# First block of a two-block network: a gate chunk moved ahead of the gated-delta drain, side work stepped later, first weight units split between two norms

## The chip, the cores and the metric

The program runs on one core of a Trainium2 chip. A core has five engines with a queue of instructions each, which run on their own and meet through semaphores: TensorE (PE; PEld is its weight load), VectorE (DVE), ScalarE (ACT), GpSimd (POOL) and SyncE (SP), which here only issues DMAs. The metric is the device time of one execution in microseconds (us); lower is better. The median over several runs counts.

## What is computed

256 tokens of width 1024 go through a first block of two layers (`first0`, `first1`), a final norm, and a second block of six phases (swiglu, hybrid mixer, swiglu, swiglu, recurrent mixer, swiglu). The change lies in the first block alone. One layer of it is, cut to what matters:

```python
h = rms_norm(x, norm_g[l])
gu, gv, gz, rq, rk, rv, rz, dq, dk, dv, dz, ab... = split(h @ w_in[l])
y_a = gmlp_branch(gu, gv, gz, ...)        # gelu, layer norm of v, mixing over tokens, gate z
y_b = retention_branch(rq, rk, rv, rz, ...)
y_c = gdn_branch(dq, dk, dv, dz, ab...)   # gated delta rule: triangular solves (I + L)^-1, states
proj  = einsum("bsnw,nwd->bsnd", stack(y_a, y_b, y_c), w_branch_out[l])
gates = sigmoid(einsum("bsd,dne->bsne", h, w_gate[l]))
x = x + sum(gates * proj, axis=2) @ w_out[l]
```

## The kernel before, in words

All weights stream through one queue of **units** of 128 x 1024 floats (`unit`, L280): SP issues the load of a unit into `st`, ACT rounds it into `wh` (L277), DVE makes the remainder `wl = st - wh` (L278). Products are made three times (`mm3`: high by high, high by low, low by high), so a unit costs 12 matmuls of 512 columns: six for each of the two token tiles. Five raw and six split units are in flight (`NS`, `NW`).

`xs` (L305) makes one chunk of 512 columns, with the tokens on the partitions: for each unit a **half unit** (six matmuls) for token tile 0 and one for tile 1. After each half unit `step` (L238) advances the **side work**: every queue of generators (`gdn`, `gm`, `ret`, `load`) by one `yield`, and functions that were put aside by `hold` for so many half units. So the place of a side instruction among the weight matmuls is counted in yields. Within each engine the instructions run in the order in which they stand; PE's, DVE's and ACT's order is made by a scheduler when the program is built, POOL's is the order in which the code is written (`tc.manual_schedule` for Pool in `run`, L538).

The first block's layer (`first`, L660) has three branches:

- **Retention**, side work in the queue `ret`. Its last step takes a power on POOL (`rsr<-rsv,mhalf` of 128 x 8, L414) for the row factors of `ro`, which DVE applies.
- **Gated MLP** (`gmlp`, L809). The chunk `v` is passed through gelu into `tB`; `mean_rstd` takes its mean and variance on DVE and a power on POOL (`rsr<-rsv,mhalf` of 128 x 1, once per token tile). The generator `mix` (queue `gm`) waits `YA` = 6 yields, normalizes `tB` on DVE, waits two yields, and multiplies by `gsw` on PE: the four matmuls `sm<-tB,gsw` per token tile, called the **gsw group** below.
- **Gated delta rule** (`gdn_core`, L969, queue `gdn`). It makes the triangular matrices L and stores their diagonal blocks (`gdl<-g`), loads them with one block per partition (`gv<-gdl`, called X), and inverts them on POOL alone, column by column: for j = 1 to 30 a product (`gtx<-gv`, L1063) and a sum (`gv<-gv,gtx`, L1065) of (31-j) x j elements, one yield per j. Then X goes out to memory (`gdt<-gv`), comes back as whole matrices (`g<-gdt`), DVE transposes these (`g<-g`, STREAM_TRANSPOSE, L1091), and PE doubles the size of the inverted blocks twice: the **g group** `gd<-g,g` (eight matmuls of 64 columns for a chunk of tokens), a mask on DVE (`gY<-gd,cst`), the **gY group** `gd<-gY,g`, a subtraction, transposes `gd<-ci,g`. Solves, states and outputs follow.

The branches' outputs meet in `merge` (L765): for a branch and a half of the columns one chunk of the gate (four units) and one chunk of the branch's projection (two units). `merge(yb, .)` is for retention, `merge(gm[3], .)` for the gated MLP, `merge(yc, .)` for the gated delta rule. `drain("gdn")` (L720) runs what is left of the side work before the chunk `dz` (`cd`), which gates that branch's output `od`; `branch_T(..., n)` transposes a branch's output n half units later.

At the start, `run` norms and transposes both token tiles, `prep(0)` and `prep(1)`, and then the weight stream begins.

Of the kernel before, what the change touches and what calls it, by code (L numbers as in the profile page):

```python
# [19 lines left out]
# half units of the weight stream before the constants are loaded, and before the use of a norm's factors  # L20
NY = 12
YA, YB = 6, 6
# column chunks of a swiglu computed with the tokens on the partitions
FX = 2
# weight units in flight: split ones, and ones as they come in
NW, NS = 6, 5
# units that the second token tile runs behind
LO, LF, LH, LR = 4, 6, 4, 5
# matmuls that bring up the tensor engine's clock
# [3 lines left out]
# columns of the constant pack  # L33
# [4 lines left out]
# rows of the broadcast pack  # L38
B_FIN, B_PN, B_LN, B_RG, B_SSM, B_IN = 0, 1, 7, 9, 11, 12
# columns of the small vector pack  # L40
V_L, V_DTB, V_ALOG, V_D, V_FB, V_N = 24, 48, 64, 80, 96, 104
# columns of the per-channel pack
# [37 lines left out]
def host_layout(i, phases=PHASES):  # L80
    i = {k: np.asarray(v) for k, v in i.items()}
    seg = []
    for ph in phases:
        if ph.startswith("first"):
# [9 lines left out]
            seg += [pieces(dz)] + mg(0, CS[1]) + mg(2, CS[0]) + mg(2, CS[1])  # L94
# [56 lines left out]
def bcl(ap, n):  # L151
    """[128, a] -> [128, a, n] along a new last axis."""
    return ap.unsqueeze(ap.ndim).to_broadcast(list(ap.shape) + [n])


def bcm(ap, n):
    """[128, a] -> [128, n, a] along a new middle axis."""
    return ap.unsqueeze(1).to_broadcast([ap.shape[0], n] + list(ap.shape[1:]))
# [10 lines left out]
class Net:  # L169
    def __init__(self, tc, a, out, phases):  # L170
        self.tc, self.nc, self.a, self.out = tc, tc.nc, a, out
        self.phases = phases
        self.wi = 0
        self.pend = deque()
        self.lag = 0
        self.bg = {}
        self.held = deque()
        self.zeroed = False
        self.ready = False

# [35 lines left out]
    def later(self, fn):  # L216
        """queue work of the second token tile, which runs `lag` units behind the first."""
# [8 lines left out]
    def spawn(self, queue, gen):  # L226
        """side work, advanced by one yield per half unit of the weight stream, in order per queue."""
        self.bg.setdefault(queue, deque()).append(gen)

    def hold(self, fn, n=3):  # L230
        """fn a few half units later, so that its matmuls don't wait for the work before them."""
# [19 lines left out]
    def turns(*gens):  # L251
        """one yield of each in turn."""
# [16 lines left out]
    def tr4(self, srcs, tag="sm"):  # L269
        """transposes of [128, 128] blocks into one bank."""  # L270
# [9 lines left out]
    def unit(self, g=None):  # L280
        """next weight unit as (hi, lo), each [128, 1024]; its rows (two k-tiles) scaled by g."""
# [23 lines left out]
    def xs(self, cb, lhs=None, nk=8):  # L305
        """one 512-column chunk; lhs(k, t) gives the (hi, lo) of k-tile k; cb(t, psum [128, 512])."""
# [20 lines left out]
    def outp(self, lhs, nk, cb):  # L327
        """all 1024 columns; cb(t, c, psum) for half c. The last units of the second token tile go by halves."""
# [27 lines left out]
    def ws(self, evac, pair=None):  # L356
        """one 512-column chunk, transposed: evac(f, psum[128 columns, 256 tokens]),
        or pair(f // 2, psum[128 columns, 2, 256]).

        Two column tiles share a bank: the first matmul into the bank clears its flags for both."""  # L360
# [25 lines left out]
    def small_proj(self, src, n, out):  # L386
        """side work: a few columns of the input projection, PSUM [128, 2, n] appended to out."""
# [21 lines left out]
    def pw(self, o, i):  # L409
        """i ** -0.5"""  # L410
# [18 lines left out]
    def prep_open(self, ph, tag="bcn"):  # L429
        """tiles for the transposed input of phase ph; returns prep(t, scratch [128, 1024]).  # L430

        A swiglu has the norm's gain in its weights, and takes the row factor when it leaves PSUM."""
# [22 lines left out]
        def prep(t, h):  # L455
# [15 lines left out]
            if ffn:  # L471
                # half the row factor, and 4 eps over its square for the norm after the swiglu
# [10 lines left out]
    def post(self, ph, half, prep, tag="h"):  # L483
        """x += (0.5 if half) * rms_norm(out, g), then the next phase's input.

        After a swiglu out still lacks its row factor, which is in the eps instead."""
# [26 lines left out]
    def log1pexp(self, x, shape, tag):  # L513
        """log(1 + exp(-|x|)) by 2 atanh(u / (2 + u)), u = exp(-|x|) <= 1."""
# [23 lines left out]
    def run(self):  # L538
        tc, nc, a = self.tc, self.nc, self.a
        with (  # L540
            # GDN's blocks take GpSimd turns with the powers of the norms, as traced
# [8 lines left out]
            # for the diagonal blocks of GDN's systems, and of their inverses in a matrix of zeros  # L550
# [12 lines left out]
            # loads the function table while x is on its way  # L563
            self.act(cp.tile([128, 1], F32, tag="first", name="first"), self.mhalf[:, :1], AF.Tanh)
            nc.sync.dma_start(self.x[0], a["x"][TS[0]])
            with tc.tile_pool(name="start", bufs=1) as self.ph:
# [3 lines left out]
                # the tensor engine's clock is up by the time x is there  # L570
                z, warm = self.t("z", [128]), self.sm()
                nc.vector.memset(z, 0.0)
                for n in range(WARM):
                    self.mm(warm[:, :128], z, z, start=True, stop=True)
                for t in range(2):
                    prep(t, self.t("h", [1024], bufs=2))
            if not self.phases[0].startswith("first"):
# [31 lines left out]
    def ffn(self, ph, nxt):  # L609
        """silu(r a) b, with the row factor r of the norm; the second r is left to the next norm."""  # L610
        self.lag = LF
        hid = []
        for c in range(FX):
            hid.append([[self.t(f"a{n}{c}{t}", [2, 128], F32R) for n in "hl"] for t in range(2)])

            def cb(t, ps, c=c):
                # silu(r a) = (tanh(r a / 2) + 1) r a / 2
# [42 lines left out]
    def first(self, l, nxt):  # L660
# [58 lines left out]
        self.merge(gm[3], m, 0)  # L719
        self.drain("gdn")  # L720
# [3 lines left out]
        def cd(t, ps):  # L724
# [6 lines left out]
            self.branch_T(yc, t, of, 14)  # L731

        self.xs(cd)
        self.merge(gm[3], m, 1)
# [30 lines left out]
    def merge(self, y, m, c, new=False):  # L765
        """m += 2 * sigmoid(gate) * (y @ w_branch_out), half c of the columns."""
# [18 lines left out]
    def silu2(self, p, tag="gate", bufs=3):  # L785
        """2 * silu of a PSUM tile."""
# [22 lines left out]
    def gmlp(self, l):  # L809
        """callbacks of the chunks u, v and z, and the branch's output."""  # L810
# [13 lines left out]
        def mix(t, mv, r):  # L824
# [3 lines left out]
            for _ in range(1 if t else YA):  # L828
# [22 lines left out]
    def rot(self, dst, w):  # L851
        """rotary embedding of a chunk of four heads, transposed into dst."""
# [116 lines left out]
    def gdn_core(self, G):  # L969
        """side work; a yield after every group of matmuls, the two chunks taking turns."""  # L970
# [11 lines left out]
        # sums of squares of q and k: [128 tokens, (q, k), chunk, head]  # L982
# [14 lines left out]
        # coefficients, [128, chunk, dir, head]  # L997
# [10 lines left out]
        # L (lower, unit diagonal left out) and masked scores P, per chunk and direction  # L1008
# [29 lines left out]
        # a diagonal block of 32 per partition: inverse of (I + block), column by column in its place  # L1038
# [12 lines left out]
        # decays over a chunk: 0: fwd to the row (incl.), 1: fwd from the row, 2, 3: mirrored  # L1051
# [5 lines left out]
        ea, eb = [ex[:, 0], ex[:, 2]], [ex[:, 1], ex[:, 3]]  # L1057
        nc.gpsimd.tensor_scalar(X, X, -1.0, None, op0=MUL)
        tx = self.t("gtx", [256])[:64]
        for j in range(1, 31):  # L1060
# [5 lines left out]
            yield  # L1066
        nc.gpsimd.memset(X.rearrange("p i j -> p (i j)")[:, ::33], 1.0)
# [3 lines left out]
        # inverses of (I + L): T = TN and its transpose TT, doubling the size of the diagonal blocks  # L1071
# [13 lines left out]
        for _ in range(3):  # L1085
# [32 lines left out]
        # solves, states and outputs  # L1118
# [430 lines left out]
```

## Time and profile before

| | us |
|---|---|
| median of 3 runs | 1747.17 |
| lowest and highest | 1743.41, 1748.79 |
| the profiled execution's span | 1749.0 |
| PE busy | 1702.5 (97%) |
| DVE busy, ACT busy | 1194.5 (68%), 884.3 (51%) |
| POOL busy | 159.3 (9%) |
| layer `first0` on the trace, about | 0 to 345 |
| layer `first1`, about | 345 to 672 |

PE is the engine that is busy nearly all the time; times with `<-` in a row name what released a waiting engine. The granted TensorE clock (PEclk) is a share of full speed: 1.00 is 2.4 GHz, 0.50 is 1.2 GHz. The mean over the span is 0.982.

### The profile page before, as it was taken

The numbers are of one execution on the slowest core, as the hardware profiler recorded it, in microseconds if no ns is written. First come the engines' busy times: TensorE is split into PE (matmuls) and PEld (weight loads), VectorE is DVE, ScalarE is ACT, GpSimd is POOL, SyncE is SP. The second block draws the span as 40 slices with busy tenths as digits, with TensorE's granted clock in tenths as the row PEclk, the third lists the DMA queues.
The fourth block names the chain that finished last, engine by engine and source line by source line (L and its number), as shares of the span: only waits on it lengthen the run. The fifth ranks groups of instructions, "written<-read, shape, count | busy, mean of one in ns | idle before, by whom it ended". The sixth has DMA issues, their size and how long they took to land.

```text
span 1749.0 us, 26736 instructions
## 1 busy us (share of the span) xinstructions
PE 1702.5 (97%) x10312; PEld 1504.4 (86%) x10312; DVE 1194.5 (68%) x1941; ACT 884.3 (51%) x1387; POOL 159.3 (9%) x207
## 2 busy tenths in 40 slices
PE   9998999999989999999999999999999999999998
PEld 8986888797878887998799888999789987979986
DVE  6887466688765667774568766865587647987743
ACT  5543244454513447553465455653475535875532
POOL 0058000001830000000000000000000000000000
PEclk9999899999979999999999999999999999999999
DMA  8455336464543455654454335754565545447542
GB/s 303 150 163 180 111 113 199 158 203 131 171 138 110 155 182 201 214 184 149 171 181 157 107 110 175 254 186 157 180 237 185 182 154 195 157 146 227 183 156 74
DMA packets 83279, 296.80 MB, mean 170 GB/s; under 512 B 9680, under 2 KB 10320, under 8 KB 83152
## 3 DMA queue, kind: packets, MB, share of 16 engines
q1 hardware_dynamic: 81360, 289.85, 49.9%
q0 software_dynamic: 1792, 5.24, 1.1%
q8 instruction: 81, 1.33, 0.3%
q14 instruction: 46, 0.38, 0.1%
HBM read 290.33 MB, written 4.72 MB: 169 GB/s over the span
## 4 chain that ended last, share of the span: by engine, by line
PE 80%; POOL 6%; DVE 5%; ACT 3%; DMA 3%; issue 2%; SPq 0%; POOLq 0%; DVEq 0%; ACTq 0%
PE mm L198 70%; PE gd L198 6%; POOL gv L1065 2%; POOL gtx L1063 2%; PE sm L273 2%; PE sm L198 2%; POOL rsr L414 1%; DMA st<-in_wst_dram 1%; DVE wl L192 1%; DVE wl L278 1%; ACT wh L277 1%; PE gd L273 1%; DVE x L192 1%; ACT wh L195 1%; DMA gdt<-gv 1%
## 5 line engine op out<-in xcount | busy, mean ns | idle before, releaser
L278 DVE TENSOR_TENSOR wl<-st,wh 128x1024 fp32r<-128x1024 f32 x348 | 430.8, 1244 | 276.3 <-ACT wh L277 275.4
L277 ACT CAST wh<-st 128x1024 fp32r<-128x1024 f32 x348 | 363.8, 1049 | 446.4 <-PE mm L198 420.0
L198 PE MATMUL mm<-hh,wh 128*128 128x256 f32 x1664 | 473.8, 285 | 0.0
L198 PE MATMUL mm<-hl,wh 128*128 128x256 f32 x1664 | 471.6, 283 | 0.0
L198 PE MATMUL mm<-hh,wl 128*128 128x256 f32 x1664 | 471.1, 283 | 0.0
L198 PEld LDWEIGHTS mm<-hh,wh 128*128 128x128 f32 x1664 | 319.1, 192 | 2.0 <-issue 1.2
L198 PEld LDWEIGHTS mm<-hl,wh 128*128 128x128 f32 x1664 | 317.4, 191 | 1.5 <-issue 1.2
L198 PEld LDWEIGHTS mm<-hh,wl 128*128 128x128 f32 x1664 | 317.4, 191 | 1.2 <-issue 1.0
L192 DVE SCALAR_TENSOR_TENSOR wl<-st,ci,wh 128x512 fp32r<-128x512 f32 x352 | 251.3, 747 | 78.7 <-ACT wh L195 78.6
L195 ACT ACTIVATE wh<-st,ci 128x512 fp32r<-128x512 f32 x352 | 234.2, 716 | 105.9 <-PE mm L198 84.2
L198 PE MATMUL mm<-wh,hh 128*128 128x512 f32 x656 | 272.2, 417 | 2.2 <-ACT wh L277 2.1
L198 PE MATMUL mm<-wh,hl 128*128 128x512 f32 x656 | 262.6, 401 | 0.0
L198 PE MATMUL mm<-wl,hh 128*128 128x512 f32 x656 | 260.1, 397 | 0.0
L198 PEld LDWEIGHTS mm<-wh,hh 128*128 128x128 f32 x656 | 125.7, 192 | 26.8 <-ACT wh L277 2.4
L198 PEld LDWEIGHTS mm<-wh,hl 128*128 128x128 f32 x656 | 125.5, 191 | 27.0 <-issue 0.5
L198 PEld LDWEIGHTS mm<-wl,hh 128*128 128x128 f32 x656 | 125.5, 191 | 24.2 <-issue 1.4
L198 PE MATMUL mm<-wl,ah 128*128 128x512 f32 x352 | 138.9, 394 | 0.0
L414 POOL TENSOR_TENSOR rsr<-rsv,mhalf 128x1 f32<-128x1 f32 (+1 forms) x32 | 29.0, 906 | 1204.4 <-DVE rsv L192 954.5
L198 PE MATMUL mm<-wh,ah 128*128 128x512 f32 x352 | 138.4, 393 | 0.0
L198 PE MATMUL mm<-wh,al 128*128 128x512 f32 x352 | 138.3, 393 | 0.0
L198 PEld LDWEIGHTS mm<-wh,ah 128*128 128x128 f32 x352 | 65.9, 187 | 15.8
L198 PEld LDWEIGHTS mm<-wh,al 128*128 128x128 f32 x352 | 65.9, 187 | 15.5
(386 smaller groups left out, 2041.9 us busy)
## 6 DMA issues: line engine op xcount, KB each, us to landing
st<-in_wst_dram SPq DMA_DIRECT2D x524, 512.0 KB, 3.5
bcp<-in_bc_dram SPq DMA_DIRECT2D x7, 512.0 KB, 5.2
gdl<-g POOLq DMA_DIRECT2D x8, 256.0 KB, 2.8
cst<-in_bc_dram SPq DMA_DIRECT2D x4, 512.0 KB, 4.8
g<-gdt POOLq DMA_DIRECT2D x8, 256.0 KB, 4.4
bcn<-in_bc_dram SPq DMA_DIRECT2D x3, 512.0 KB, 5.4
x<-in_x_dram SPq DMA_DIRECT2D x2, 512.0 KB, 4.9
cst<-in_cst_dram SPq DMA_DIRECT2D x4, 256.0 KB, 4.6
```

Source lines behind the costliest of these rows:

```text
L192: self.nc.vector.scalar_tensor_tensor(o, a, s, b, op0=op0, op1=op1)
L195: self.nc.scalar.activation(o, i, f, **k)
L198: self.nc.tensor.matmul(*a, **k)
L273: self.nc.tensor.transpose(p[:, j], s, self.ident)
L277: self.nc.scalar.copy(hi, src)
L278: self.nc.vector.tensor_sub(lo, src, hi)
L414: self.nc.gpsimd.tensor_tensor(o, i, self.mhalf[:, :i.free_size()], op=ALU.pow)
L1063: nc.gpsimd.tensor_tensor(u, X[:, j + 1:, j:j + 1].to_broadcast([64, n, j]), X[:, j:j + 1, :j].to_broadcast([64, n, j]), op=MUL)
L1065: nc.gpsimd.tensor_tensor(X[:, j + 1:, :j], X[:, j + 1:, :j], u, op=ADD)
```

## The change

It does six things, in both layers except for the last:

1. The second gate and projection of the gated MLP, `merge(gm[3], m, 1)`, come before `drain("gdn")` and the chunk `dz` instead of after them (the weight stream's order on the host follows).
2. `gdn_core` yields ten times more: three times before the first POOL instruction on X, once after each odd j with (31-j) x j over 200 (j = 11, 13, ... 21: six), and once more before `chain`.
3. `mix` waits 10 yields instead of 6 (`YA`), and 2 instead of 1 for the second tile.
4. The transposes of the third branch's output are held 5 half units instead of 14.
5. The docstrings and comments go (left out below).
6. At the very start, three weight units are loaded and split after `prep(0)` and before `prep(1)`; `unit` hands them out later.

```diff
-YA, YB = 6, 6
+YA, YB = 10, 6
...
-            seg += [pieces(dz)] + mg(0, CS[1]) + mg(2, CS[0]) + mg(2, CS[1])
+            seg += mg(0, CS[1]) + [pieces(dz)] + mg(2, CS[0]) + mg(2, CS[1])
...
+        self.pre = deque()
...
     def unit(self, g=None):
+        if self.pre:
+            return self.pre.popleft()
...
+                self.ui = self.xn = 0
                 for t in range(2):
                     prep(t, self.t("h", [1024], bufs=2))
+                    if t == 0 and self.phases[0].startswith("first"):
+                        first = [self.unit() for _ in range(3)]
+                self.pre.extend(first)
...
         self.merge(gm[3], m, 0)
+        self.merge(gm[3], m, 1)
         self.drain("gdn")
...
-            self.branch_T(yc, t, of, 14)
+            self.branch_T(yc, t, of, 5)
 
         self.xs(cd)
-        self.merge(gm[3], m, 1)
         self.merge(yc, m, 0)
...
-            for _ in range(1 if t else YA):
+            for _ in range(2 if t else YA):
                 yield
...
         ea, eb = [ex[:, 0], ex[:, 2]], [ex[:, 1], ex[:, 3]]
+        for _ in range(3):
+            yield
         nc.gpsimd.tensor_scalar(X, X, -1.0, None, op0=MUL)
...
             nc.gpsimd.tensor_tensor(X[:, j + 1:, :j], X[:, j + 1:, :j], u, op=ADD)
             yield
+            if n * j > 200 and j % 2:
+                yield
...
-        for _ in range(3):
+        for _ in range(4):
             yield
 
         def chain(c):
```

Where the instructions stand is shown for three places of `first0`; `first1` has the same pattern (its first power stands after j = 9 before and after j = 6 now, its two other ones follow j = 17 now).

POOL, inversion of X: `gtx` is the product and `gv` the sum of one j, and the free sizes give (31-j) x j; `rsr` of 128 x 8 is retention's power, `rsr` of 128 x 1 the gated MLP's. Before, retention's stands after j = 8 and the gated MLP's first one after j = 22:

```order
L1063 TENSOR_TENSOR gtx<-gv 64x184
L1065 TENSOR_TENSOR gv<-gv,gtx 64x23x8
L414 TENSOR_TENSOR rsr<-rsv,mhalf 128x8
L1063 TENSOR_TENSOR gtx<-gv 64x198
...
L1063 TENSOR_TENSOR gtx<-gv 64x198
L1065 TENSOR_TENSOR gv<-gv,gtx 64x9x22
L414 TENSOR_TENSOR rsr<-rsv,mhalf 128x1
L1063 TENSOR_TENSOR gtx<-gv 64x184
```

Now the same engine and place:

```order
L1074 TENSOR_TENSOR gv<-gv,gtx 64x26x5
L417 TENSOR_TENSOR rsr<-rsv,mhalf 128x8
L1072 TENSOR_TENSOR gtx<-gv 64x150
...
L1072 TENSOR_TENSOR gtx<-gv 64x240
L1074 TENSOR_TENSOR gv<-gv,gtx 64x15x16
L417 TENSOR_TENSOR rsr<-rsv,mhalf 128x1
L1072 TENSOR_TENSOR gtx<-gv 64x238
```

Retention's power moved forward to behind j = 5, the gated MLP's first one to behind j = 16.

PE, the side groups among the weight matmuls (`mm<-...`, left out as "..."), from the first gsw group to the first g groups. Before:

```order
L198 MATMUL sm<-tB,gsw 128x128 x4
...
L273 MATMUL gd<-ci,g_635 128x128 x2
...
L198 MATMUL sm<-tB,gsw 128x128 x4
...
L198 MATMUL gd<-g_1765,g_979 128x64 x4
L198 MATMUL gd<-g_1767,g_985 128x64 x4
...
L198 MATMUL gd<-gY,g_1675 128x64 x4
```

Now:

```order
L199 MATMUL sm<-tB,gsw 128x128 x4
...
L274 MATMUL gd<-ci,g_635 128x128 x2
...
L199 MATMUL gd<-g_1867,g_979 128x64 x4
L199 MATMUL gd<-g_1869,g_985 128x64 x4
...
L199 MATMUL gd<-g_1883,g_1055 128x64 x4
L199 MATMUL gd<-g_1885,g_1061 128x64 x4
...
L199 MATMUL gd<-gY,g_1773 128x64 x4
```

The first gsw group stands 24 weight matmuls later than before, and from it to the first g group there are now 78 weight matmuls, two gsw and two transpose groups (before: 47 weight matmuls and the same four groups). In `first1` these are 24 and 72.

DVE, from the transposes of the inverses to the first mask `gY`. Before:

```order
L1091 STREAM_TRANSPOSE g_1765<-g_1675 128x512
L1091 STREAM_TRANSPOSE g_1767<-g_1677 128x512
L1091 STREAM_TRANSPOSE g_1782<-g_1679 128x512
L278 TENSOR_TENSOR wl<-st,wh 128x1024
L1091 STREAM_TRANSPOSE g_1784<-g_1681 128x512
L183 TENSOR_TENSOR gY<-gd,cst 128x512
```

Now:

```order
L1102 STREAM_TRANSPOSE g_1885<-g_1779 128x512
L279 TENSOR_TENSOR wl<-st,wh 128x1024
L193 SCALAR_TENSOR_TENSOR gate<-gate,mm 128x512
L184 TENSOR_TENSOR ggm<-gv,grv 128x512
L193 SCALAR_TENSOR_TENSOR tA<-tA,gate 128x512
L193 SCALAR_TENSOR_TENSOR gate<-gate,mm 128x512
L279 TENSOR_TENSOR wl<-st,wh 128x1024
L193 SCALAR_TENSOR_TENSOR tA<-tA,gate 128x512
L279 TENSOR_TENSOR wl<-st,wh 128x1024
L184 TENSOR_TENSOR ggm<-gv,grv 128x512
L184 TENSOR_TENSOR gY<-gd,cst 128x512
```

The mask now stands behind three weight splits and six other instructions that follow the transposes (before: one weight split, among the transposes).

## Rows read from the trace of the kernel before

**Rows 1.** Waits of PE over the span: total us, times, longest us.

```profile
PE sm L198 <- issue: 11.4, 2, 6.7
PE gd L198 <- DVE g L1091: 9.7, 2, 6.0
```

**Rows 2.** Timeline of PE in `first0`: start, us, instruction [idle before].

```profile
150.67 0.39 PE L198 MATMUL mm<-wh,hl 128*128 128x512 f32 x1
157.77 2.05 PE L198 MATMUL sm<-tB,gsw 128*128 128x128 f32 x8 [6.71 <-issue]
...
166.57 1.05 PE L198 MATMUL sm<-tB,gsw 128*128 128x128 f32 x8
...
178.88 3.65 PE L198 MATMUL gd<-g,g 128*128 128x64 f32 x16 [6.02 <-DVE g L1091]
...
200.33 0.60 PE L273 MATMUL gd<-ci,g 128*128 128x128 f32 x4
```

**Rows 3.** Chain of waits in order of time, PE: start, us, instruction.

```profile
202.32 1.73 PE gd L198 x16
...
249.59 32.96 PE mm L198 x144
```

**Rows 4.** Timeline of PE in `first1`.

```profile
481.92 0.60 PE L273 MATMUL gd<-ci,g 128*128 128x128 f32 x4
...
506.33 3.65 PE L198 MATMUL gd<-g,g 128*128 128x64 f32 x16 [3.69 <-DVE g L1091]
...
533.10 1.89 PE L198 MATMUL gd<-g,g 128*128 128x64 f32 x16
```

**Rows 5.** Windows: span, PE, PEld, DVE, ACT, POOL, granted clock, DMA.

```profile
520.00:526.00 6.00, 6.00 (x23) 5.31 (x24) 1.89 (x3) 0.97 (x1) 0.00 (x0) 0.50 0.00 0
```

**Rows 6.** Timeline of POOL in `first0`.

```profile
118.51 0.46 POOL L1065 TENSOR_TENSOR gv<-gv,gtx 64x130 f32<-64x130 f32 x1
...
139.34 1.56 POOL L1065 TENSOR_TENSOR gv<-gv,gtx 64x240 f32<-64x240 f32 x1
...
149.49 0.56 POOL L1063 TENSOR_TENSOR gtx<-gv 64x210 f32<-64x210 f32 x1
...
166.75 2.58 POOL L1070 DMA_DIRECT2D gdt<-gv  x4 [0.29 <-POOL gv L1067]
```

**Rows 7.** Timeline of DVE in `first0`.

```profile
121.64 0.52 DVE L189 TENSOR_SCALAR rsv<-rmv 128x8 f32<-128x8 f32 x1
...
147.01 0.15 DVE L189 TENSOR_SCALAR rsv<-bn 128x1 f32<-128x1 f32 x1
...
152.53 0.72 DVE L189 TENSOR_SCALAR tB<-tB,bn,rsr 128x512 f32<-128x512 f32 x1 [4.09 <-POOL rsr L414]
...
178.03 2.09 DVE L1091 STREAM_TRANSPOSE g<-g 128x512 f32<-128x512 f32 x3 [1.22 <-DMA g<-gdt]
```

**Rows 8.** Timeline of POOL in `first1`.

```profile
447.67 0.48 POOL L1065 TENSOR_TENSOR gv<-gv,gtx 64x150 f32<-64x150 f32 x1
...
453.01 1.67 POOL L414 TENSOR_TENSOR rsr<-rsv,mhalf 128x8 f32<-128x8 f32 x1 [0.27 <-DVE rsv L189]
...
469.17 1.51 POOL L1065 TENSOR_TENSOR gv<-gv,gtx 64x238 f32<-64x238 f32 x1
...
494.19 2.58 POOL L1070 DMA_DIRECT2D gdt<-gv  x4 [0.29 <-POOL gv L1067]
```

**Rows 9.** Timeline of DVE in `first1`.

```profile
476.77 0.15 DVE L189 TENSOR_SCALAR rsv<-bn 128x1 f32<-128x1 f32 x1
```

**Rows 10.** Timeline of DVE at the start.

```profile
11.69 0.74 DVE L192 SCALAR_TENSOR_TENSOR h<-x,rsr,bcn 128x512 f32<-128x512 f32 x1
...
12.95 1.22 DVE L278 TENSOR_TENSOR wl<-st,wh 128x1024 fp32r<-128x1024 f32 x1
```

**Rows 11.** Timeline of ACT and DVE, chunk `dz` of `first0`.

```profile
264.76 0.60 ACT L195 ACTIVATE gate<-mm 128x512 f32<-128x512 f32 x1 [0.30 <-PE mm L198]
...
267.55 0.68 DVE L183 TENSOR_TENSOR g<-g,gate 128x512 f32<-128x512 f32 x1
```

## The prediction

> **What bounds the kernel now.** I read the waits of PE first, then PE's timeline around the long ones, then what releases them on POOL and DVE. PE is busy 97% of the span, so a gain comes from its idle time or from its clock. Two kinds of waits carry most of its idle time [rows 1]: 11.4 us before gsw groups and 9.7 us before g groups, each twice, once per layer. The trace gives "issue" as the releaser of the first kind. Its true cause stands on DVE: the normalization of `tB` starts at 152.53 after 4.09 us of waiting for POOL's power [rows 7], and PE's gsw group starts at 157.77 [rows 2]. POOL was no faster because it runs the inversion of X in between. The second kind is the inversion's own end: X leaves POOL at 166.75 [rows 6], and 12.1 us later, after two DMAs and a transpose, the g group starts at 178.88 [rows 2]. In `first1` the same way takes 494.19 to 506.33, again 12.1 us [rows 4, 8]. After each wait PE runs at half clock for some time: 0.50 still between 520 and 526 us [rows 5], and a g group takes 3.65 us there instead of 1.73 [rows 2, 3].
>
> So the loss of a layer is idle time plus slow clock. I take it as time less work, and work as counts times full-speed durations: a weight matmul 32.96 / 144 = 0.229 us and a group of eight gd matmuls 1.73 us [rows 3], a transpose group 0.60 and a gsw group 1.05 us [rows 2]. In `first0` from 150.9 (end of the last weight matmul issued before the wait) to 200.33 there are, by the order, 84 weight matmuls, 4 g or gY groups, 5 transpose groups and 2 gsw groups: 19.2 + 6.9 + 3.0 + 2.1 = 31.2 us of work in 49.4 us, **18.2 us lost**. In `first1` from 481.92 to 533.10: the same with 6 transpose groups, 31.8 us in 51.2, **19.4 us lost**. Of these, 4.2 us (178.88 to 200.33: 21.4 less 17.2 of work) and 9.0 us (506.33 to 533.10: 26.8 less 17.8) come after the release of the g group. All of it together is 37.6 us, and that is all that this change can win there.
>
> **The change part by part: when PE comes to the g group.** The matmuls of `merge(gm[3], m, 1)` are only moved, none is added; what counts is where side groups stand among them. The first gsw group comes 24 weight matmuls later: 150.9 + 24 x 0.229 = 156.4 us. By then `tB` is ready: the power comes earlier (below), and DVE needs some 6 us from it to the end (152.53 to 157.77 before, with one weight split more now). So the wait of 6.71 us goes, and in `first1` that of 4.7 (the rest of the 11.4), at 481.9 + 5.5 = 487.4. From there to the g group stand 78 weight matmuls, two gsw and two transpose groups: 17.9 + 2.1 + 1.2 = 21.2 us, so PE arrives at 177.6; in `first1`, with 72, at 487.4 + 19.8 = 507.2. Against the old releases of 178.88 and 506.33 the second wait would nearly be gone too.
>
> **When the g group is released.** Here the extra yields bite, and it decides the sum. POOL keeps the written order, so when the inversion's steps come later in the stream, the powers stand earlier among the steps, and POOL waits for their inputs. In `first0` retention's power follows j = 5, which ended at 118.97 [rows 6]; its input is there at 121.64 + 0.52 = 122.2 [rows 7], since nothing on its way moved. POOL idles 3.3 us. The gated MLP's first power follows j = 16, which ended at 139.34 + 1.56 = 140.9, now 144.2; its input came at 147.2 [rows 7], now about 1.1 us earlier, since DVE gets retention's factors that much sooner: 1.9 us idle. Together 5.2 us. In `first1` retention's power follows j = 6, which ended at 448.15, and its input came just ahead of 453.01, where POOL had waited 0.27 us for it already [rows 8]: 4.9 less 0.3. The steps j = 7 to 9 then come after it, which puts the end of j = 17 from 470.7 to 475.2, and the gated MLP's input comes at 476.9 [rows 9]: 1.8 us. The two powers now stand side by side, and the second input is made on DVE after the first power's result: 1.5 us more (a power, one DVE instruction of 0.7 and a short one, as at 152.53). Together 7.9 us.
>
> To this I add 1.5 us in each layer, because the later steps lose a quiet time of DVE: a sum of j = 16 took 1.56 us, a product of j = 21 only 0.56 us at 149.49, when DVE stood idle [rows 6, 7]. This is an estimate; its ends are 0 (the steps meet as many DVE instructions as before) and 4.4 (they all meet them at the rate of the 11 us before 166.75). With it the release is at 178.9 + 6.7 = 185.6 and 506.3 + 9.4 = 515.7. **PE waits 8.0 us (185.6 less 177.6) and 8.5 us (515.7 less 507.2).** One wait per layer is left of two, longer than each.
>
> **After the release.** The mask `gY` now stands behind three weight splits and six other instructions on DVE. With 0.70 us for a transpose (2.09 / 3) [rows 7] and about as much for the others, 1.22 for a split [rows 10], the mask is done at most 10.5 us after PE's first g group (1.9 + 3 x 1.22 + 7 x 0.70). PE has 6.2 us of work until the gY group at full clock (12 weight matmuls, two g groups) and 12.4 at half. So 4.3 us are lost there at least, by the mask or by the clock, and the two hide each other. I take 4.5 us, nearest to the 4.2 of `first0`, where matmuls stood as densely; the upper end is the 9.0 of `first1`. New loss: 8.0 + 8.5 + 2 x 4.5 = 25.5 us, a gain of 12.1.
>
> **The start.** The first weight split on DVE stands at 12.95 behind a half norm and a split that started at 11.69 [rows 10]; these two now come later. PE's first dense stretch can begin 1.26 us sooner, at half clock at first. The second tile's late split could take that back. Between 0 and 1.3 I take 1.0, nearer to the rows.
>
> **Edits at nothing.** The transposes of `od` come 5 half units after the chunk `dz`, 24 weight matmuls or 5.5 us after tile 0's last matmul. ACT starts 0.30 us after that matmul (264.46), and `od` is ready at 268.23 [rows 11]: 3.8 us. The following matmuls cover it; if DVE is behind, each layer loses what is over, 1 to 2 us. ACT waits with its copies into `gv` for X's DMA as before, but three weight units are now split ahead of them, so PE does not come to miss one before the g group. The ten yields cost nothing on any engine themselves.
>
> **The sum.** 12.1 + 1.0 = 13.1 us off the profiled execution's 1749.0, which is 1.8 us over the median. The other runs have the same stalls, so I take the same off the median: **1747.2 - 13.1 = 1734.1 us**.
>
> **Rivals.** *POOL isn't held by the powers* (their inputs come sooner than I read). Then the releases stay at 178.9 and 506.3, the idle time is 1.3 and 0 us, some 4.3 us each are lost to the mask, and 27.7 + 1.0 us are won: 1718.5. For it speaks that the input of `first1`'s first power is seen only by the end of POOL's wait; against it that this wait, 0.27 us, was there at all, with three more steps ahead of it [rows 8]. Chance 0.10.
>
> *The clock stays low* after the longer waits, as it did after 506.33: 9.0 us lost in each layer after the release instead of 4.5. Then the gain is 4.1: 1743. For it: the only wait left is longer than any before. Against it: in `first1` before, PE stood with few weight matmuls between its small groups, and now there are six after each. Chance 0.17.
>
> *Slower: POOL's steps are stretched by DVE.* The 26 instructions of j = 18 to 30 cost 1.0 us more whenever they are slow (1.56 against 0.56) [rows 6]; I read six slow ones before. If DVE's dense work after the earlier powers makes two in three slow, that is 11 more per layer, 9.5 us beyond my 1.5, twice: 1747.2 - 13.1 + 19 = 1753. From 6.5 us per layer on, the gain is gone. Against it: DVE's work itself is not more than before. Chance 0.11. The Trainium skill, page "SBUF — State Buffer", section "Who interferes with whom", has a rule that points this way: VectorE and GpSimd share a port pair as an exclusive lock, and a GpSimd instruction that meets a VectorE one with two SBUF inputs, as a weight split is, blocks until that one's end. By that rule each of the 26 could wait for up to a whole split; the trace agrees as far as the quick row at 149.49 stands in DVE's idle time and the slow one does not.
>
> **How the numbers follow.** The forecast has 0.62, with a range of its own from 1728 to 1741. A measurement of this kernel can tell about 0.3%, 5.2 us, from no change. Faster by more (under 1742): 0.57 of the forecast, all of the first rival, 0.03 of the second, together 0.70. Within: 0.05, 0.13 and 0.02 of the third, 0.20. Slower: 0.10. The range reaches to the first rival's edge and past the second, 1719 to 1747, and leaves out the half of the first and most of the third.
>
> **What would show it.** On PE no wait before a gsw group, and one before a g group in each layer of 7 to 10 us. On POOL idle time ahead of the powers, 3.3 and 1.9 us in `first0`, 4.9, 1.8 and 1.5 in `first1`, and X leaving POOL 5 to 9 us later. On DVE the mask some 10 us after the transposes start. At the start, the first weight split near 11.7 us. The prediction is wrong if POOL shows no such idle time, if PE waits elsewhere (before the transposes of `od`, or for a weight unit), or if the slow clock lasts 20 us after each release.

## The result and the profile after

The changed kernel takes **1728.69 us** (median of four runs, 1726.01 to 1729.85) against 1747.98 for the kernel before, run beside it: a ratio of 0.9891 (95% interval 0.9877 to 0.9906), 19.3 us less. The profiled executions differ by 21.3 us (1749.0 and 1727.7). PE's granted clock over the span rose from 0.982 to 0.99.

Where it was won is seen from the first transposes of a layer's result on PE. Start, duration and instruction, before:

```profile
339.04 0.63 PE L273 MATMUL sm<-ci,r 128*128 128x128 f32 x4 [0.51 <-DVE r L192]
670.84 0.63 PE L273 MATMUL sm<-ci,x 128*128 128x128 f32 x4 [0.51 <-DVE x L192]
```

and after:

```profile
330.40 0.63 PE L274 MATMUL sm<-ci,r 128*128 128x128 f32 x4 [0.51 <-DVE r L193]
651.00 0.63 PE L274 MATMUL sm<-ci,x 128*128 128x128 f32 x4 [0.51 <-DVE x L193]
```

8.6 us were won by the end of `first0` and 11.2 more by the end of `first1`, 19.8 in all; the 1.5 us left lie in phases that the change doesn't touch, and runs of one kernel differ by more than that.

Of the two long waits of [rows 1] one is left. Waits of PE after (us in total, times, longest):

```profile
PE gd L199 <- DVE g L1102: 10.6, 2, 5.5
```

PE's timeline after, around the g groups of `first0` and then of `first1` (answers to [rows 2] and [rows 4]):

```profile
155.84 1.05 PE L199 MATMUL sm<-tB,gsw 128*128 128x128 f32 x8
...
176.08 0.39 PE L199 MATMUL mm<-wh,hl 128*128 128x512 f32 x1
181.52 3.65 PE L199 MATMUL gd<-g,g 128*128 128x64 f32 x16 [5.05 <-DVE g L1102]
...
187.63 3.51 PE L199 MATMUL gd<-g,g 128*128 128x64 f32 x16
...
193.60 1.93 PE L199 MATMUL gd<-gY,g 128*128 128x64 f32 x16
...
199.99 0.60 PE L274 MATMUL gd<-ci,g 128*128 128x128 f32 x4
...
503.12 3.64 PE L199 MATMUL gd<-g,g 128*128 128x64 f32 x16 [5.55 <-DVE g L1102]
...
519.65 0.60 PE L274 MATMUL gd<-ci,g 128*128 128x128 f32 x4
```

The first gsw group starts with no idle time ahead of it. PE comes to the g group at 176.47 and 497.57 (start less idle time) and waits 5.05 and 5.55 us. A g group of 3.65 us is at half clock (1.2 GHz), one of 1.9 at full.

POOL after, the places where the powers stand among the steps of the inversion, both layers (answers to [rows 6] and [rows 8]):

```profile
118.56 0.46 POOL L1074 TENSOR_TENSOR gv<-gv,gtx 64x130 f32<-64x130 f32 x1
121.00 1.67 POOL L417 TENSOR_TENSOR rsr<-rsv,mhalf 128x8 f32<-128x8 f32 x1 [1.97 <-DVE rsv L190]
122.65 0.47 POOL L1072 TENSOR_TENSOR gtx<-gv 64x150 f32<-64x150 f32 x1
...
144.97 0.56 POOL L417 TENSOR_TENSOR rsr<-rsv,mhalf 128x1 f32<-128x1 f32 x1
...
163.23 2.58 POOL L1072 TENSOR_TENSOR gtx<-gv 64x150 f32<-64x150 f32 x1
...
171.96 2.58 POOL L1081 DMA_DIRECT2D gdt<-gv  x4 [0.29 <-POOL gv L1078]
...
443.47 1.67 POOL L417 TENSOR_TENSOR rsr<-rsv,mhalf 128x8 f32<-128x8 f32 x1 [3.86 <-DVE rsv L190]
...
467.73 0.56 POOL L417 TENSOR_TENSOR rsr<-rsv,mhalf 128x1 f32<-128x1 f32 x1
469.01 1.47 POOL L417 TENSOR_TENSOR rsr<-rsv,mhalf 128x1 f32<-128x1 f32 x1 [0.72 <-DVE rsv L190]
...
493.51 2.58 POOL L1081 DMA_DIRECT2D gdt<-gv  x4 [0.29 <-POOL gv L1078]
```

POOL does wait for the inputs of retention's power (1.97 and 3.86 us) and hardly for the gated MLP's. X leaves at 171.96 instead of 166.75.

DVE after, `first0` (answers to [rows 7]):

```profile
120.75 0.17 DVE L190 TENSOR_SCALAR rsv<-rmv 128x8 f32<-128x8 f32 x1
122.70 4.77 DVE L190 TENSOR_SCALAR ro<-ro,rmv,rsr 128x128 f32<-128x128 f32 x8 [1.79 <-POOL rsr L417]
...
143.86 0.15 DVE L190 TENSOR_SCALAR rsv<-bn 128x1 f32<-128x1 f32 x1
...
163.15 2.35 DVE L279 TENSOR_TENSOR wl<-st,wh 128x1024 fp32r<-128x1024 f32 x2
...
180.66 0.71 DVE L1102 STREAM_TRANSPOSE g<-g 128x512 f32<-128x512 f32 x1 [12.99 <-DMA g<-gdt]
...
190.76 0.68 DVE L184 TENSOR_TENSOR gY<-gd,cst 128x512 f32<-128x512 f32 x1
```

The DMA engines in the 4 us from X's store on, both layers. The columns are the stretch, its length, the busy time of PE, PEld, DVE, ACT and POOL, the granted clock, the DMA engines' busy share and GB/s. Before:

```profile
166.75:170.75 4.00, 4.00 (x23) 3.43 (x23) 3.18 (x7) 0.00 (x0) 2.58 (x4) 1.00 0.95 297
494.19:498.19 4.00, 4.00 (x24) 3.40 (x23) 2.64 (x4) 1.05 (x1) 2.58 (x4) 1.00 0.99 344
```

After:

```profile
171.96:175.96 4.00, 4.00 (x19) 3.30 (x19) 0.00 (x0) 0.00 (x0) 2.57 (x4) 1.00 0.51 63
493.51:497.51 4.00, 4.00 (x18) 3.01 (x17) 0.00 (x0) 0.00 (x0) 2.57 (x4) 1.00 0.52 66
```

Before, X's store met weight loads, 297 and 344 GB/s in all; after, it met next to none, since X's own 64 x 1024 floats make 66 GB/s over 4 us. X came 5 us later, when ACT and DVE (0.00 busy) took no more units and stood waiting for it; that their waiting stopped the loads is not shown (see e8). From the store's issue to PE's g group it took 12.13 and 12.14 us before and 9.56 and 9.61 after.

### The profile page after: what moved, and what is told of

Read it like the earlier page. It is cut to its first block, busy times and chain, and to the rows that moved or that the text cites. A ratio compares the mean times of both kernels' runs of the same rounds, so it can differ in the third digit from the quotient of the medians.

```text
span 1727.7 us, 26747 instructions
## 1 busy us (share of the span) xinstructions
PE 1690.8 (98%) x10312; PEld 1494.8 (87%) x10312; DVE 1194.8 (69%) x1941; ACT 883.2 (51%) x1387; POOL 165.1 (10%) x207
## 4 chain that ended last, share of the span: by engine, by line
PE 81%; POOL 7%; DVE 4%; ACT 3%; DMA 2%; issue 2%; SPq 0%; POOLq 0%; DVEq 0%; ACTq 0%
PE mm L199 71%; PE gd L199 6%; POOL gtx L1072 3%; POOL gv L1074 2%; PE sm L199 2%; PE sm L274 2%; POOL rsr L417 1%; DMA st<-in_wst_dram 1%; DVE wl L193 1%; ACT wh L278 1%; DVE wl L279 1%; PE gd L274 1%; DVE x L193 1%; ACT wh L196 1%; ACT h L196 0%
```

## Experiments

Ratios are to the kernel before, run on the same chip in turn with each; the changed kernel itself has 0.9891 (0.9877 to 0.9906).

| run | what it is | median us | ratio (95%) |
|---|---|---|---|
| e3 | before, moved merge alone | 1750.6 | 1.0014 (0.9998 to 1.0030) |
| e2 | after, without the ten yields | 1753.9 | 1.0046 (1.0029 to 1.0062) |
| e9 | after, merge back | 1731.0 | 0.9899 (0.9884 to 0.9914) |
| e7 | after, `YA` back | 1730.7 | 0.9903 (0.9887 to 0.9919) |
| e10 | after, hold back | 1728.4 | 0.9889 (0.9875 to 0.9903) |
| e4 | after, start back | 1728.9 | 0.9897 (0.9879 to 0.9916) |
| e1 | after, nine yields behind X | 1732.0 | 0.9912 (0.9890 to 0.9934) |
| e11 | after, mask ahead of splits | 1726.4 | 0.9873 (0.9854 to 0.9892) |
| e5 | both of these | 1718.6 | 0.9831 (0.9814 to 0.9847) |
| e6 | e5, own buffer for v | 1723.3 | 0.9854 (0.9826 to 0.9882) |
| e12 | e5, two more yields | 1716.6 | 0.9826 (0.9807 to 0.9846) |
| e8 | after, own buffer for v | 1729.9 | 0.9898 (0.9878 to 0.9917) |

### Which part of the change makes the gain

**e3**, from the kernel before:

```diff
-            seg += [pieces(dz)] + mg(0, CS[1]) + mg(2, CS[0]) + mg(2, CS[1])
+            seg += mg(0, CS[1]) + [pieces(dz)] + mg(2, CS[0]) + mg(2, CS[1])
...
         self.merge(gm[3], m, 0)
+        self.merge(gm[3], m, 1)
         self.drain("gdn")
...
-        self.merge(gm[3], m, 1)
         self.merge(yc, m, 0)
```

> The kernel before (1748) with the moved merge alone. Theory: side groups are counted in half units, so PE's order up to the g groups is the same and both waits stay; only the dz chunk and what follows come later: 1745 to 1750, no change. Rival: the moved merge alone is the gain: 1730 to 1738.

No gain, as the theory had it. Waits of PE in e3:

```profile
PE sm L198 <- issue: 11.2, 2, 6.6
PE gd L198 <- DVE g L1091: 9.9, 2, 6.0
```

Both waits of [rows 1] are there, 11.2 and 9.9 us for 11.4 and 9.7.

**e2**, from the kernel after (as all that follow):

```diff
-        for _ in range(3):
-            yield
         nc.gpsimd.tensor_scalar(X, X, -1.0, None, op0=MUL)
...
-            if n * j > 200 and j % 2:
-                yield
...
-        for _ in range(4):
+        for _ in range(3):
             yield
```

> The changed kernel without the ten extra yields in gdn_core; the moved merge, YA = 10, the shorter hold and the start stay. Theory: the yields are what moves the g groups behind the moved merge's matmuls; without them PE comes to the first g group after 54 weight matmuls from the first gsw group's old place, near 166 us, and waits 10 to 13 us in each layer for X, about what both waits of the kernel before took together; the slow clock after it stays: 1742 to 1746. Rival: the moved merge and the later gsw groups carry the gain without the yields: 1728 to 1733.

Without the yields the other parts lose 0.46% against the kernel before. PE's timeline in e2, the first g group of each layer:

```profile
177.50 1.94 PE L199 MATMUL gd<-g,g 128*128 128x64 f32 x8 [13.64 <-DVE g L1098]
...
509.70 1.94 PE L199 MATMUL gd<-g,g 128*128 128x64 f32 x8 [12.69 <-DVE g L1098]
```

26.3 us of waiting against 21.1 in [rows 1]. I had put the waits at 10 to 13 us and the time 8 to 12 us lower: the sign of the theory was right, the size wasn't. The gsw groups, which stand later, no longer have a wait of their own, and the whole lateness of X is met at once.

**e9**:

```diff
-            seg += mg(0, CS[1]) + [pieces(dz)] + mg(2, CS[0]) + mg(2, CS[1])
+            seg += [pieces(dz)] + mg(0, CS[1]) + mg(2, CS[0]) + mg(2, CS[1])
...
         self.merge(gm[3], m, 0)
-        self.merge(gm[3], m, 1)
         self.drain("gdn")
...
+        self.merge(gm[3], m, 1)
         self.merge(yc, m, 0)
```

> The changed kernel (1728.7) with the gated MLP's second merge back behind the drain and the chunk dz; yields, YA, hold and start as in the change. Theory 'the moved merge is cover for the end of the side work': the g groups keep their place, but the solves and states, later by ten yields, run in the drain with four groups in a row and no weight matmuls between; each link of that chain costs 1 to 2 us on DVE or ACT: 4 to 8 us per layer, 1736 to 1745. Rival 'the merge is not needed, the yields alone make the gain': 1728 to 1731.

My theory fell: the interval overlaps that of the change, so the moved merge, named first in the title, is worth too little to be told from nothing. The side work that the drain runs without cover is short: the only wait of PE in e9 of a kind that the changed kernel doesn't have is 0.2 us for the mask `gY`.

**e7**:

```diff
-YA, YB = 10, 6
+YA, YB = 6, 6
...
-            for _ in range(2 if t else YA):
+            for _ in range(1 if t else YA):
                 yield
```

> The changed kernel (1728.7) with the gsw groups back at their old place (6 yields and 1 instead of 10 and 2). Theory 'the wait for X absorbs what comes before it': the normalization of tB now ends near 152 us, so PE waits some 2 to 3 us before the first gsw group, comes that much later to the g group and waits that much less there; only a short slow clock after the extra wait is lost, if it isn't absorbed too: 1728 to 1731. Rival 'the later gsw groups carry part of the gain': both old waits of 6.7 and 4.7 us come back, 1735 to 1740.

The time is as expected; the wait before the first gsw group is 1.0 us and not the 2 to 3 of the theory. Waits of PE in e7:

```profile
PE gd L199 <- DVE g L1102: 8.6, 2, 5.1
...
PE sm L199 <- PE mm L199: 1.6, 2, 1.0
```

1.6 us before the gsw groups come back, and 2.0 us go from the wait for X: what is ahead of that wait is absorbed by it. The power that ended the old 6.7 us is early now because the yields moved it, not because the gsw group waits for it later.

**e10** (`self.branch_T(yc, t, of, 14)` again) and **e4** (no units split between the norms):

```diff
-                    if t == 0 and self.phases[0].startswith("first"):
-                        first = [self.unit() for _ in range(3)]
-                self.pre.extend(first)
```

> The changed kernel (1728.7) with the transposes of the third branch held 14 half units again instead of 5. Theory: the hold costs nothing at 5, and at 14 PE meets the merge of the third branch before its transposes are due, so the last of them run uncovered there: 1729 to 1732. Rival 'no effect': 1728 to 1729.5.

> The changed kernel without the three weight units that are split between the two norms at the start. Theory: PE's first dense stretch starts 1.1 us later and everything after it too: 1729.5 to 1730.5, 1.0 to 1.5 us above the changed kernel. Rival: the start is hidden again by the waits for X in both layers, whose releases do not depend on it: 1728 to 1729.

Neither can be told from the change. In e4 PE's first g group starts at 182.27 instead of 181.52, but in e9 and e10, which keep the start, it does at 181.93 and 181.81: what the start is worth is not to be seen here either. Undone one at a time, the yields are the only one of the edits that is missed. No run has the yields alone on the kernel before, so that they need none of the others is not shown.

### What holds the g group, and what is late next

**e1**: nine yields (three ahead of the inversion, six in it) put behind it.

```diff
-        for _ in range(3):
-            yield
         nc.gpsimd.tensor_scalar(X, X, -1.0, None, op0=MUL)
...
-            if n * j > 200 and j % 2:
-                yield
...
-        for _ in range(4):
+        for _ in range(13):
             yield
```

> The changed kernel (1728.7 us), with nine of gdn_core's ten extra yields (three before the inversion, six in it) moved behind it, so that on POOL the powers stand after the same steps as in the kernel before, while PE comes to the g groups at the same count of weight matmuls as in the changed kernel. Theory 'the powers hold X': the inversion leaves POOL some 5 us sooner in first0 (about 166.8) and 7 us sooner in first1 than in the changed kernel; with 9.6 to 12.1 us to the g group the waits of 5.0 and 5.5 us shrink to 0 to 2.5, and the half clock after them with them: 1711 to 1719. Rival 'the way back is what is late': the DMAs out and back take 12 us or more because weight loads run beside them, waits stay at 3 to 4 us: 1722 to 1726. Rival 'DVE and ACT': the transposes and the copies into gv now stand ahead of weight splits and hold them: PE waits for wl instead, 1729 or more.

X comes sooner and the time does not: 0.9912 against 0.9891. Waits of PE in e1:

```profile
PE gd L199 <- DVE gY L184: 7.8, 2, 5.3
...
PE gd L199 <- DVE g L1098: 1.4, 2, 0.9
```

and DVE's timeline in `first0`:

```profile
177.76 0.71 DVE L1098 STREAM_TRANSPOSE g<-g 128x512 f32<-128x512 f32 x1 [1.28 <-DMA g<-gdt]
...
182.34 2.32 DVE L279 TENSOR_TENSOR wl<-st,wh 128x1024 fp32r<-128x1024 f32 x2
...
186.50 1.22 DVE L279 TENSOR_TENSOR wl<-st,wh 128x1024 fp32r<-128x1024 f32 x1
...
188.24 1.22 DVE L279 TENSOR_TENSOR wl<-st,wh 128x1024 fp32r<-128x1024 f32 x1
189.37 0.68 DVE L184 TENSOR_TENSOR gY<-gd,cst 128x512 f32<-128x512 f32 x1
```

X leaves POOL at 167.17 and the wait for the transposes is down from 10.6 to 1.4 us: that half of the theory holds. Then PE waits 7.8 us for the mask, which stands on DVE behind the transposes, five weight splits and other work, 11.6 us after the first transpose. I had named a third rival that had PE wait for `wl`; it was the mask. The yields in the wrong place were a delay that another delay hid.

**e11** is the change with the mask ahead of the splits, **e5** is e1 with it:

```diff
-        if g is None:
+        self.nmask -= 1
+        if g is None and 0 <= self.nmask < 6:
+            self.nc.scalar.copy(hi, st)
+            with self.tc.issue_after(self.mask):
+                self.nc.vector.tensor_sub(lo, st, hi)
+        elif g is None:
             self.split(hi, lo, st)
...
-                self.tt(y, p1, mask)
+                ins = nc.vector.tensor_tensor(y, p1, mask, op=MUL).ins
+                if lv == 0 and c == 0:
+                    self.mask, self.nmask = ins, 8
```

(in e11 `7` for `8`). `issue_after` only orders DVE's queue.

> The changed kernel (1728.7), with the weight splits after the next one queued behind the first mask gY on DVE; the yields stay in the inversion. Theory 'X's late release hides the mask': after the 5.0 and 5.5 us of waiting PE runs at half clock and comes to the gY group after the mask anyway, so the order edge alone gives nothing: 1727 to 1730. Rival 'the mask's place alone is the gain of the run with both': 1717 to 1721.

> The kernel with nine yields behind the inversion (1732.0 us), and on DVE an order edge: of the weight splits after the g groups all but two queue behind the first mask gY instead of ahead of it. Theory 'the mask in DVE's queue ate what the earlier inversion gave': in that kernel PE waits 2.6 us in first0 and 5.3 us in first1 for gY, and runs at half clock twice; with two splits (2.4 us) less ahead of it the mask is done near 187 when PE comes at 187.4, the wait and the second slow stretch go: 6 us in first0 and 8 in first1, 1716 to 1721. Rival 'the splits are needed too': PE waits for wl right behind the gY groups instead, 1728 to 1734.

Alone, each has an interval that overlaps that of the change; both together give 0.9831, 10 us less than the change. Waits of PE in e5 and its two gY rows:

```profile
PE gd L200 <- DVE g L1104: 2.4, 3, 1.2
```

```profile
187.16 1.89 PE L200 MATMUL gd<-gY,g 128*128 128x64 f32 x16
...
501.66 2.00 PE L200 MATMUL gd<-gY,g 128*128 128x64 f32 x16 [0.52 <-DVE gY L1116]
```

The mask's wait is down from 7.8 to 0.5 us. With X late (e11) the order edge had little to win, but not for the reason of my theory, that PE comes to the gY group at half clock. In the profiled run of e11, the fastest of its four, PE is at full clock from the second g group on in both layers, and the mask is done 2.7 and 2.5 us before PE comes. PE and DVE in `first0` of e11:

```profile
186.87 1.89 PE L200 MATMUL gd<-g,g 128*128 128x64 f32 x16
190.04 1.89 PE L200 MATMUL gd<-gY,g 128*128 128x64 f32 x16
...
186.70 0.68 DVE L1120 TENSOR_TENSOR gY<-gd,cst 128x512 f32<-128x512 f32 x1
```

In e4, e7, e9 and e10 the mask stands where the change has it and the second g group of `first0` is at full clock too; there PE waits 0.2 to 1.0 us for the mask, in e1 2.6 and 5.3. So with X late the mask costs a microsecond at most, and with X early its place decides.

**e6** and **e8**: the copies of v go into the two `gdl` buffers instead of X's buffer (e6 from e5, e8 from the change).

```diff
-        gv = self.t("gv", [2, 4, 128])
...
-            vt.append(gv[:, c])
+            vt.append(self.t("gdl", [4, 128], bufs=2))
```

> As the run before, and the copies of v no longer go into the buffer that the inversion X uses (into the two gdl buffers instead), so ACT doesn't wait 12 us for X's DMA with weight units behind it. Theory 'ACT's wait holds splits back': units are rounded while X is on its way, the products with grv on DVE stand before the transposes, and the mask comes 1.3 us sooner: 1714 to 1719. Rival 'weight loads slow the way back': ACT's wait was what kept the loads off the DMA engines; now they run beside X's store and load, the way back takes 12 us and more instead of 10 to 11.5, and it is no better than the run before: 1718 to 1724.

> The changed kernel (1728.7) with the copies of v in the two gdl buffers instead of X's buffer, nothing else. Theory 'weight loads lengthen the way back': in the changed kernel ACT waits for X, rounding stops, the raw buffers fill, the DMA engines are idle from 168 us on and X comes back in 9.6 us (12.1 before, when loads ran at 380 to 420 GB/s). With ACT free, two or three more loads run then: the way back takes 10.5 to 12 us and PE waits 6 to 7.5 us for each g group: 1730 to 1734. Rival 'the way back does not depend on the loads': waits stay at 5.0 and 5.5 us: 1726 to 1729.

Both are inconclusive. The intervals of e6 and e5 overlap. e8 was to bring weight loads back beside X's store, and didn't: 77 and 68 GB/s in the 4 us from the store, a way back of 9.67 and 10.17 us. So it doesn't test what it was made for. It does show that the loads stop without ACT's wait for X: in `first0` of e8 ACT rounds three units from 171.03 on, and of the two only DVE stands waiting for X, from 167.6 to 179.74. Nor were the DMA engines idle from 168 us on in the change, as that theory has it; they moved 232 GB/s from 168 to 172 us.

**e12**: e5 with 15 instead of 13 yields behind the inversion.

> The fastest kernel so far (nine yields behind the inversion, mask ahead of the splits, 1718.6) with two yields more behind the inversion, so that PE comes to the first g group 12 weight matmuls (2.7 us) later. Theory: its remaining waits for the transposes (1.2 and 0.6 us in first0, 0.9 and 0.7 in first1) go and with them the slow clock that follows (2 to 3 us per layer): 1710 to 1715. Rival 'the end of the side work gets uncovered or the splits run out': 1718 to 1722.

In the profiled run, the fastest of five, the g groups no longer wait, and PE's clock stays at 1.00 around them in both layers, but most of the 4 to 9 us that I expected did not come. Waits of PE in e12 and one of the two places:

```profile
PE mm L200 <- DVE wl L280: 4.5, 2, 3.1
```

```profile
178.78 0.50 PE L200 MATMUL mm<-wl,hh 128*128 128x512 f32 x1 [1.37 <-DVE wl L280]
```

The split of the next unit stands behind the first transpose, which waits for X on DVE: that is the rival's "splits run out". e12 and e5 can't be told apart; both beat the change and the kernel before.

## Why the prediction was right, point by point

1734.1 was forecast and 1728.7 measured: right in sign and inside the range, at the very edge of the forecast's own 1728 to 1741, and 13.1 us of gain stood against 19.3 us measured.

- **Arrival.** 177.6 forecast, 176.47 measured. Of the 1.1 us, half came in the stretch from the gsw group (155.84) to the g group, 20.6 us for 21.2, and half is a lead of 0.6 us that PE had by 94 us: `gd<-gk` starts at 93.56, in the kernel before at 94.17. The first weight split does start at 11.59 instead of 12.95, as forecast, but e9, with the same start, has no such lead (94.46), so the start's 1.0 us is not shown. The wait before the gsw group is gone, as forecast, but e7 shows that the later groups are not the reason.
- **The powers hold POOL.** Right for retention's: 1.97 us for 3.3 (122.2 less 118.97 is 3.2; and the input came 1.2 us sooner, at 120.92, half of it by PE's lead and half by shorter instructions on DVE just ahead, while the inversion started no sooner), and 3.86 for 4.6. Wrong for the gated MLP's: 0 and 0.7 us for 1.9 and 3.3. Its input was ready at 144.0, 3.2 us sooner than before, where I had allowed 1.1; DVE had started `ro` with retention's factors 2.4 us sooner (122.70 for 125.08).
- **Stretched steps.** Estimated at 1.5 us with ends 0 and 4.4. From the first product to X's store it is 57.98 us after and 52.80 before; 1.97 of the 5.18 between is the wait, so 3.2 us are steps that took longer. In `first1`, 60.68 less 53.23 less 4.31 of waits: 3.1. The rows show the meeting: the 64x150 product took 2.58 us at 163.23, beside two weight splits on DVE (163.15, 2.35 us), and 0.47 us at 122.65, with no split beside it. The Trainium skill, page "SBUF — State Buffer", section "Who interferes with whom", says that a DVE instruction with two SBUF inputs contends with a GpSimd instruction that reads SBUF; the two rows agree. While DVE ran `ro` (one tensor with row factors, from 122.70 on) POOL's eight steps took 0.47 to 0.58 us each, but DVE itself was slow there. One `ro` took 680 ns in the mean over both layers, another TENSOR_SCALAR of 128x128 (`fs<-fs,fsu`) 285. So it may be that these meet too and DVE is the one that waits; no run tests that apart.
- **The way back.** This is the term that was mis-sized: I kept 12.1 us from X's store to the g group, and it took 9.6. With 1.5 us less on POOL it puts the release of `first0` at 181.5 instead of 185.6, and with PE 1.1 us sooner the wait is 5.05 instead of 8.0; in `first1` it is 5.55 instead of 8.5. Both lie under the 7 to 10 us named as a sign. On POOL two errors partly cancelled, which is luck: 3.2 and 3.6 us less of waiting for the powers, and 1.7 and 1.6 more of stretched steps. That the waits' 5.9 us are close to the 6.2 us that the forecast was short by is chance too: 1.15 us more than forecast were lost after the release, and more was won than the sum below finds.
- **After the release.** From the g group to the first transposes behind the gY groups there are 24 weight matmuls and four groups, 12.4 us of work by [rows 3]. It took 18.47 us in `first0` and 16.53 in `first1`: 6.05 and 4.1 us lost for 4.5 each. (The "at least" 4.3 us of the prediction was no floor: it came from a mask done "at most" 10.5 us after, which bounds the mask's part from above.) The mask was done 9.9 us after PE's g group started (181.52 to 191.44), forecast at 10.5 at most.
- **Sum.** Lost in the layers: 5.05 + 6.05 + 5.55 + 4.1 = 20.8 us, forecast 25.5, before 37.6. That makes 16.8 us of gain, with PE's lead of 0.6 us 17.4; 19.8 were won by the end of `first1`. Of the 2.4 us between, 0.5 stand before the transposes `sm<-ci,tA` of `first1` (a wait of 1.39 us before, 0.90 after); the rest is not traced. The prediction's 1.8 us from 1749.0 to the median compare a span with device times, which are 1.8 us above the spans in the runs of the kernel before; nothing in its sum hangs on that.
- **Rivals.** *POOL isn't held* fell by the two waits of retention's power. *The clock stays low* came half true: in `first0` of the profiled run the half clock lasted until 193.6, 12 us. *Steps stretched by DVE* had the right mechanism at a third of its price, 3.2 us instead of 11.

What I didn't see ahead: e1 and e5 show that the late X and the late mask hid each other. The prediction priced both, and its sentence that "the two hide each other" was said of the mask and the clock; that taking one away would give nothing was not drawn from it.

## What to carry to other kernels

Where an engine's order is as written, a `yield` put in to place one engine's work also moves that engine's neighbours in time: look at every queue that the generator issues to, and put the delay behind the last instruction that must be early (here behind the inversion, not in it). A wait that is taken away shows the next one in the queue; before it is taken away, list what stands ahead of the consumer's next input on the other engine, and mend both at once (neither e1 nor e11 can be told from the change, e5 is 10 us faster). When a round trip through memory is priced by its time at another moment, compare what the DMA engines carried then and what they will carry now: here 12.1 us became 9.6.

## What the runs showed of the hardware

**X's way back is longer with loads beside it.** In all fourteen kernels and both layers, X's store and load took 8.6 to 9.6 us to the first transpose where the DMA engines moved 63 to 82 GB/s, the store itself included, in the 4 us from the store's issue (the change, e4, e7 to e11), and 10.5 to 12.6 where they moved 259 to 387 (before, e1 to e3, e5, e6, e12). That they go together is shown; that the loads are the cause was not tested apart, since e8 left the loads as they were. The Trainium skill, page "DMA: Bandwidth & Descriptors", section "Queues, rings and completion order", says of DMAs issued by SP and ACT that a completion's semaphore increment lands only after every earlier write of that DMA engine, across its queues. X's DMAs are issued by POOL, and no run here tells such an order from shared bandwidth.

**The half clock after nearly the same wait lasted 6 us in one run and 12 in another.** The change and e10 have the same order up to there, and waits of 5.05 and 4.89 us. Windows of `first0` (columns as above), the change:

```profile
182.00:187.00 5.00, 5.00 (x20) 4.61 (x20) 4.89 (x8) 0.93 (x1) 0.00 (x0) 0.50 0.28 79
188.00:193.00 5.00, 5.00 (x20) 4.61 (x20) 5.00 (x7) 0.00 (x0) 0.00 (x0) 0.50 0.58 193
```

and e10:

```profile
182.00:187.00 5.00, 5.00 (x20) 4.68 (x21) 4.95 (x8) 1.14 (x2) 0.00 (x0) 0.50 0.24 75
188.00:193.00 5.00, 4.42 (x33) 3.82 (x33) 5.00 (x7) 1.05 (x1) 0.00 (x0) 1.00 0.55 177
```

Over six runs with waits of 4.6 to 5.05 us in `first0`, the second g group is at half clock in two (the change and e8, 3.51 us) and at full in four (e4, e9, e10 and e11, 1.89 to 2.03). At full clock again, e10's PE waits 0.57 us for the mask; from the g group to the gY group it takes 9.93 us instead of the change's 12.08. So a fifth of what the faster clock gives (0.57 of 2.72) is taken back: the slow clock and DVE's queue cover each other in part, as the prediction had it.
